# First mixer's input projection cut along K into 4, 5 and 7 tiles for every piece, with earlier parts written back into PSUM by ScalarE

## The chip, the core and the metric

One core of one Trainium2 chip runs the whole program. The metric is the device time of one execution in microseconds (us), lower is better. PE stands for TensorE, DVE for VectorE, ACT for ScalarE, POOL for GpSimd and SP for SyncE, whose queue issues nearly all loads.

## What is computed

Two decoder layers over 256 tokens of width 2048, batch 1, all in fp32. Each mixer and each feed-forward part starts from a normalised and modulated input, and the modulation is itself a matrix product with the conditioning vector `c`:

```python
cond = jax.nn.silu(c)
for i in range(DEPTH):                                   # 2 layers
    mod = (cond @ w_mod[i] + b_mod[i])[:, None, :]       # w_mod[i] is 2048 x 12288
    sh_m, sc_m, g_m, sh_f, sc_f, g_f = jnp.split(mod, 6, axis=-1)
    h = rmsnorm(x, norm_mix[i]) * (1.0 + sc_m) + sh_m
    y = gla_mixer(h, ...) if i % 2 == 0 else fox_mixer(h, ...)
    x = x + (1.0 + g_m) * y
    h = rmsnorm(x, norm_ffn[i]) * (1.0 + sc_f) + sh_f
    x = x + (1.0 + g_f) * conv_ffn(h, ...)
return rmsnorm(x, norm_final)

def gla_mixer(h, w_in, w_gate, b_gate, g_norm, w_out):   # the first mixer
    q, k, v, r, a = split(h @ w_in, widths 1024, 1024, 2048, 2048, 16)
    log_alpha = log_sigmoid(a @ w_gate + b_gate) / 16
    ...                                                  # chunked gated linear attention over q, k, v
    return (rmsnorm(o) * silu(r)) @ w_out
```

So the first mixer cannot multiply K rows 128k to 128k+127 of `w_in` before the same rows of `sc_m` and `sh_m` are known, and those need the matching columns of `w_mod`: 1 MB of `w_mod` for each of the two, for each of the 16 tiles of K.

## The kernel before

A weight tile is 128 rows of K by 1024 columns, 512 KB. Every tile goes the same way: SP loads it into the `ring` pool, ACT writes its rounded copy `wh` (L120), DVE writes the remainder `wl` (L124), and PE multiplies it in three products, `wh` by the high part of `h`, `wh` by its low part, `wl` by the high part: 24 matmuls of 256 columns (L602 to L604, the function `stream_a`), or 12 of 512 columns for the pieces `v0` and `v1` (L638 to L640, `stream_b`). `wh` and `wl` have AHEAD + 1 = 4 buffers each. So the cast of tile n waits until PE has finished tile n - 4, and at most three tiles wait converted.

`make_h` produces one K tile of `h`: DVE multiplies `x` by the token scale (L517), ACT writes the high part (L518), DVE computes the same affine in fp32 (L519) and subtracts (L520) for the low part. The modulation is summed on DVE, a multiply-add for each 128 rows of `w_mod` (L266, L268, `mod_tasks`, queued in `bg` and spread over the tiles by `set_pace`), then transposed, reduced and added up by a small matmul (L278, L279, L295, L311). For the first four K tiles of `h` it is summed on PE instead (`early_sum`, L1246, `early_finish`, L1252 and L1255), so that the first mixer can start; while PE waits for those loads it runs matmuls on the constant `fill` (L1283).

The first mixer's input projection (`gla`, `gla_rest`) has seven pieces: q, k, v0, v1, r0, r1 of 1024 columns and the narrow piece a of 16. Along K it runs in this order: q, k, v0 over K tiles 0 to 3; then `finish_late`, which sums `sh_m` for tiles 4 to 7 on PE; then q, k, v0 over tiles 4 to 7; then a, v1, r0, r1 over tiles 0 to 7; then all seven over tiles 8 to 15. PSUM has six banks in the pool `psA` for them, a piece takes four. When a piece has run a block, `fold` moves its four banks to SBUF: the first time ACT copies them, later DVE adds them to what is there.

Engines run their instructions in program order. The order on each engine is set by a scheduler from the order in the code and the dependences; `tc.issue_after` pins an instruction behind another. `psM` is a pool of two more PSUM banks for everything small.

Of the kernel before, what the change touches and what calls it, by code (L numbers as in the profile page):

```python
# [18 lines left out]
P = 128  # L19
# [16 lines left out]
SLOAD = 12  # L36
BACK = 1
STAGE = 3
FREE = 0
PEND = 3  # L40
BLOCKS = (8, 8)
HEAD = 4
HEADED = ('q', 'k', 'v0')
# [10 lines left out]
GP0 = 0.7  # L54
# [3 lines left out]
N0, N5 = 4, 5  # L58
BG0, BG1 = 0.95, 0.45
# [13 lines left out]
def kernel(  # L73
# [20 lines left out]
    order = {"v": None, "t": None}  # L94
# [20 lines left out]
    def split_w(src, moving, after=None):  # L115
# [4 lines left out]
        nc.scalar.copy(out=hi, in_=src)  # L120
# [71 lines left out]
    nc.vector.tensor_scalar_mul(vec[:, r0["qn"]:r0["qn"] + 1], vec[:, r0["qn"]:r0["qn"] + 1], float(P) ** -0.5)  # L192
# [40 lines left out]
    startup = {"loads": [], "left": SLOAD}  # L233

    def after_startup(on=True):
        es = ExitStack()
        if on and startup["left"] > 0 and len(startup["loads"]) >= BACK:
            startup["left"] -= 1
            es.enter_context(tc.issue_after(startup["loads"][-BACK]))
        return es  # L240

    def mod_tasks(l, key, f0=0, fn=D, wide=False, defer=False, turn=False):
# [8 lines left out]
        def chunk(c0, kt, st):  # L251
            def load():
                st[kt] = bigt([P, per, width], "wm") if wide else ringt([P, per, width], "wm")
                src = w_mod[l, kt * P:(kt + per) * P, s * D + c0:s * D + c0 + width]
                with after_startup():
                    nc.sync.dma_start(out=st[kt], in_=src.rearrange("(k p) m -> p k m", p=P))
# [241 lines left out]
    def make_h(l, kind):  # L498
# [12 lines left out]
        def make(m):  # L511
# [7 lines left out]
            nc.vector.tensor_scalar(out=t, in0=t, scalar1=sc, scalar2=sh, op0=ALU.mult, op1=ALU.add)  # L519
# [31 lines left out]
    def next_w(kt, cols, hold=None):  # L551
# [4 lines left out]
        if i < STAGE:  # L556
            run, look = min(run, STAGE - i), 1
        split_to(min(i + 1 + run, len(plan)), look)
        return splits.popleft()

    def split_to(end, look=LOOK):
        while fetched["split"] < end:
            while fetched["load"] < min(fetched["split"] + look, len(plan)):
# [4 lines left out]
                for c0, cn in cols_:  # L568
                    if nk_ == 1:
                        with after_startup():  # L570
                            nc.sync.dma_start(out=wt[:, o:o + cn], in_=w_[kt_ * P:(kt_ + 1) * P, c0:c0 + cn])
                        o += cn
                    else:
                        nc.sync.dma_start(out=wt[:, :nk_ * cn].rearrange("p (k r) -> p k r", r=cn),
                                          in_=w_[kt_ * P:(kt_ + nk_) * P, c0:c0 + cn]
                                          .rearrange("(k p) r -> p k r", p=P))
# [16 lines left out]
    def stream_a(kts, cols, rhs, done=None):  # L593

        ps = banks()
        held = []

        def mms(m, k, wh, wl, rh, rl):
            first, last = k == kts[0], k == kts[-1]
# [6 lines left out]
        for k in kts:  # L606
# [6 lines left out]
            for m in range(8):  # L613
                mms(m, k, wh, wl, rh, rl)
# [12 lines left out]
    def stream_b(kts, c0, lhs):  # L627
        ps = [b.rearrange("p j t -> p (j t)") for b in banks()]
        for k in kts:
            lh, ll = lhs(k)  # L630
            wh, wl = next_w(k, [(c0, 1024)])
            first, last = k == kts[0], k == kts[-1]
            for tt in range(TT):
                ts_ = slice(tt * P, (tt + 1) * P)
                for hf in range(2):
                    hs_ = slice(hf * 512, (hf + 1) * 512)
                    o = ps[tt * 2 + hf]
                    nc.tensor.matmul(o, lh[:, ts_], wh[:, hs_], start=first, stop=False)  # L638
                    nc.tensor.matmul(o, ll[:, ts_], wh[:, hs_], start=False, stop=False)  # L639
                    nc.tensor.matmul(o, lh[:, ts_], wl[:, hs_], start=False, stop=last)  # L640
# [45 lines left out]
    def gla(l, h, finish_late):  # L686
# [3 lines left out]
        def piece(key, kts, c0):  # L690
            if key == "a":
                return narrow(kts, c0, RANK, h)
            if key[0] == "v":
                return stream_b(kts, c0, h)
            return [p.rearrange("p j t -> p (j t)") for p in stream_a(kts, [(c0, 1024)], h)]

        def fold(key, ps):
# [9 lines left out]
            new = key not in parts  # L707
            if new:
                parts[key] = bigt([P, 4, 512], key)
            for b in range(4):  # L710
                dst = parts[key][:, b, :]
                if new:
                    nc.scalar.copy(out=dst, in_=ps[b])
                else:
                    nc.vector.tensor_tensor(out=dst, in0=dst, in1=ps[b], op=ALU.add)
# [6 lines left out]

        run(HEADED, ALL[:HEAD])
        drain_bg()
        finish_late()
        run(HEADED, ALL[HEAD:BLOCKS[0]])
        run([key for key, _ in pieces if key not in HEADED], ALL[:BLOCKS[0]])
        drain_bg()
        kts = ALL[BLOCKS[0]:]
        return kts, pieces, piece, fold, parts  # L730

    def gla_rest(l, kts, pieces, piece, fold, parts):
# [3 lines left out]
        nc.sync.dma_start(out=wg[RANK:RANK + 1, :], in_=gla_b_gate)  # L736
# [646 lines left out]
```

## Time and profile before

| | |
|---|---|
| time, median of 3 runs | 2430.47 us (2429.18 to 2430.49) |
| the profiled execution | 2429.0 us, of which the span of the trace 2427.0 us |
| first matmul of the first mixer | 43.66 us after the start of the span |
| PE busy, over the span | 98% |
| DVE, ACT busy | 79%, 52% |
| mean granted TensorE clock | 0.994 |

All times of the trace count from the start of the span. A PE that is shown as busy is not a PE at its peak, since matmuls are pipelined: at full clock the matmuls of 256 columns start every 0.113 us although each is shown with 0.28 us, so 24 of them, a tile, take 2.72 us. An idle time in brackets stands before the instruction, with what ended it.

### The profile page before, as it was taken

Reading aid. Unit: us, or ns where it says so; the run is one execution under the profiler, and the core shown is the slowest. Engines: PE = TensorE matmul, PEld = TensorE weight load, DVE = VectorE, ACT = ScalarE, POOL = GpSimd, SP = SyncE. Lnnn points to the kernel's source line nnn. Section 1 sums busy time; section 2 is a strip of 40 time slices with the busy share of each in tenths; the row PEclk is TensorE's granted clock in tenths of the full one; section 3 lists DMA queues with packets and bytes.
Section 4 is the critical chain, followed back from the end, with each engine's and each line's share of the span. In section 5 each row is a group of like instructions: output and inputs, shape, how many; then the busy total and the mean of one; then the engine's idle time right before and its main releaser. Section 6 shows DMA issues by size and latency. Waiting matters only on the chain.

```text
span 2427.0 us, 46850 instructions
## 1 busy us (share of the span) xinstructions
PE 2384.6 (98%) x19127; PEld 2285.0 (94%) x19131; DVE 1922.6 (79%) x2609; ACT 1252.4 (52%) x1671; POOL 16.2 (1%) x35
## 2 busy tenths in 40 slices
PE   6999999899999999999999999999999999999998
PEld 4898899899999999999988889999999999999998
DVE  4898989888789999986687998877776767777544
ACT  4447454445556665543454455545555555565433
POOL 0000000000000000000000000000000000000000
PEclk9999999999999999999999999999999999999999
DMA  9986968898668988998589887686777777756552
GB/s 376 374 303 222 328 223 312 297 343 293 195 200 297 318 305 311 326 315 314 164 298 314 299 272 251 215 296 228 235 235 228 240 227 236 232 195 217 191 191 104
DMA packets 188148, 638.31 MB, mean 263 GB/s; under 512 B 23705, under 2 KB 24715, under 8 KB 187548
## 3 DMA queue, kind: packets, MB, share of 16 engines
q1 hardware_dynamic: 186968, 634.12, 76.9%
q8 instruction: 149, 2.44, 0.4%
q10 hardware_dynamic: 964, 1.20, 0.1%
q14 instruction: 67, 0.55, 0.1%
HBM read 633.14 MB, written 2.10 MB: 262 GB/s over the span
## 4 chain that ended last, share of the span: by engine, by line
PE 95%; DVE 3%; DMA 1%; ACT 1%; issue 1%; DVEq 0%; SPq 0%
PE pa L604 25%; PE pa L603 25%; PE pa L602 25%; PE pa L640 5%; PE pa L639 5%; PE pa L638 5%; DMA wm<-in_w_mod_dram 1%; DVE wl L124 1%; PE pe L1246 0%; PE pm L473 0%; DVE acc L268 0%; PE pm L846 0%; PE pm L868 0%; PE pm L1057 0%; PE pt L288 0%
## 5 line engine op out<-in xcount | busy, mean ns | idle before, releaser
L120 ACT CAST wh<-w 128x1024 fp32r<-128x1024 f32 x819 | 856.4, 1049 | 1001.8 <-PE pa L603 707.9
L124 DVE TENSOR_TENSOR wl<-w,wh 128x1024 fp32r<-128x1024 f32 x819 | 995.8, 1218 | 408.8 <-ACT wh L120 403.6
L603 PE MATMUL pa<-h,wh 128*128 128x256 f32 x3584 | 990.8, 278 | 3.9 <-DVE h L520 3.9
L602 PE MATMUL pa<-h,wh 128*128 128x256 f32 x3584 | 987.7, 278 | 2.1 <-ACT h L518 2.1
L604 PE MATMUL pa<-h,wl 128*128 128x256 f32 x3584 | 987.3, 278 | 1.2 <-DVE wl L124 1.2
L603 PEld LDWEIGHTS pa<-h,wh 128*128 128x128 f32 x3584 | 675.3, 189 | 5.1 <-DVE h L520 4.9
L602 PEld LDWEIGHTS pa<-h,wh 128*128 128x128 f32 x3584 | 672.3, 188 | 4.9 <-ACT h L518 2.3
L604 PEld LDWEIGHTS pa<-h,wl 128*128 128x128 f32 x3584 | 672.8, 189 | 1.6 <-DVE wl L124 1.5
L603 PE MATMUL pa<-op,wh 128*128 128x256 f32 x1920 | 526.3, 276 | 0.0
L602 PE MATMUL pa<-op,wh 128*128 128x256 f32 x1920 | 526.3, 277 | 0.0
L604 PE MATMUL pa<-op,wl 128*128 128x256 f32 x1920 | 518.5, 276 | 0.3 <-DVE wl L124 0.3
L268 DVE SCALAR_TENSOR_TENSOR acc<-wm,cT,acc 128x1024 f32<-128x1024 f32 (+1 forms) x345 | 433.2, 1256 | 1.0 <-DMA wm<-in_w_mod_dram 0.3
L603 PEld LDWEIGHTS pa<-op,wh 128*128 128x128 f32 x1920 | 360.5, 188 | 0.0
L602 PEld LDWEIGHTS pa<-op,wh 128*128 128x128 f32 x1920 | 360.2, 188 | 0.0
L604 PEld LDWEIGHTS pa<-op,wl 128*128 128x128 f32 x1920 | 355.4, 188 | 0.5 <-DVE wl L124 0.5
L639 PE MATMUL pa<-wh,h 128*128 128x512 f32 x512 | 200.2, 392 | 0.0
L638 PE MATMUL pa<-wh,h 128*128 128x512 f32 x512 | 198.0, 391 | 0.0
L640 PE MATMUL pa<-wl,h 128*128 128x512 f32 x512 | 189.5, 393 | 0.0
L638 PEld LDWEIGHTS pa<-wh,h 128*128 128x128 f32 x512 | 96.1, 188 | 19.4 <-issue 0.2
L640 PEld LDWEIGHTS pa<-wl,h 128*128 128x128 f32 x512 | 95.9, 188 | 19.5
L639 PEld LDWEIGHTS pa<-wh,h 128*128 128x128 f32 x512 | 96.1, 188 | 19.0
L1109 ACT ACTIVATE y<-u,cw 128x256 f32<-128x256 f32 x176 | 101.6, 599 | 6.7 <-DVE act L1125 4.1
(263 smaller groups left out, 1315.0 us busy)
## 6 DMA issues: line engine op xcount, KB each, us to landing
wm<-in_w_mod_dram SPq DMA_DIRECT2D x320, 512.0 KB, 5.2
w<-in_ffn_w_up_dram SPq DMA_DIRECT2D x320, 512.0 KB, 4.5
w<-in_ffn_w_down_dram SPq DMA_DIRECT2D x176, 512.0 KB, 4.4
w<-in_fox_w_in_dram SPq DMA_DIRECT2D x128, 512.0 KB, 5.2
w<-in_gla_w_in_dram SPq DMA_DIRECT2D x96, 512.0 KB, 6.0
wm<-in_w_mod_dram SPq DMA_DIRECT2D x32, 1024.0 KB, 10.7
w<-in_gla_w_out_dram SPq DMA_DIRECT2D x32, 512.0 KB, 5.5
w<-in_ffn_w_up_dram SPq DMA_DIRECT2D x64, 256.0 KB, 4.5
```

Source lines behind the costliest of these rows:

```text
L120: nc.scalar.copy(out=hi, in_=src)
L124: order["v"] = nc.vector.tensor_tensor(out=lo, in0=src, in1=hi.bitcast(F32), op=ALU.subtract).ins
L268: nc.vector.scalar_tensor_tensor(out=st["a"], in0=wt[:, j, :], scalar=col, in1=st["a"], op0=ALU.mult, op1=ALU.add)
L602: nc.tensor.matmul(o, wh[:, ms], rh, start=(first and m % 2 == 0), stop=False, skip_group_check=True)
L603: nc.tensor.matmul(o, wh[:, ms], rl, start=False, stop=False, skip_group_check=True)
L604: nc.tensor.matmul(o, wl[:, ms], rh, start=False, stop=last, skip_group_check=True)
L638: nc.tensor.matmul(o, lh[:, ts_], wh[:, hs_], start=first, stop=False)
L639: nc.tensor.matmul(o, ll[:, ts_], wh[:, hs_], start=False, stop=False)
L640: nc.tensor.matmul(o, lh[:, ts_], wl[:, hs_], start=False, stop=last)
L1109: nc.scalar.activation(y, u, AF.Identity, scale=cw[:, l * 3 + 2, r:r + 1], bias=cw[:, 6 + l, r:r + 1])
```

## The change

Every piece now runs all three blocks of K, of 4, 5 and 7 tiles: q, k, v0, v1, r0, r1, a in the first two blocks, q, a, k, v0, v1, r0, r1 in the third. In the second and third block a piece starts by ACT copying its parts from SBUF into the four PSUM banks (`preload`); the matmuls accumulate on them, and `fold` is an ACT copy every time. The first two tiles of such a piece run over the first two banks, then over the other two. `sh_m` of tiles 4 to 7 is no longer summed on PE: the modulation of the next block is summed on DVE during the block before, must be drained one tile before its end, and the first `h` of the next block are requested behind its last wide tile (`hooks`). The two token loads go first, the loads of SP are chained in code order (`sync_load`), the transposes of the small vectors and of `b_mod` move behind the token sum. In `make_h` the fp32 affine of K tiles 3 and up is done by ACT (L532) instead of DVE, in all four places where `h` is made. Some numbers of pace change with it.

```diff
-SLOAD = 12
-BACK = 1
+SLOAD = 48
 STAGE = 3
+NEAR = 20
-BLOCKS = (8, 8)
+BLOCKS = (4, 5, 7)
 HEAD = 4
-HEADED = ('q', 'k', 'v0')
+STARTS = (0, 4, 9, 16)
+ORDERS = (("q", "k", "v0", "v1", "r0", "r1", "a"),) * 2 + (("q", "a", "k", "v0", "v1", "r0", "r1"),)
-GP0 = 0.7
+GP0 = 0.8
-N0, N5 = 4, 5
-BG0, BG1 = 0.95, 0.45
+EASE, N5 = 3, 5
+BG0, BG1 = 0.95, 0.75
...
+    def sync_load(out, in_):
+        with ExitStack() as es:
+            if startup["left"] > 0 and startup["last"] is not None:
+                startup["left"] -= 1
+                es.enter_context(tc.issue_after(startup["last"]))
+            startup["last"] = nc.sync.dma_start(out=out, in_=in_).ins
...
             hot = nc.scalar.activation(hi, t, AF.Identity, scale=sc, bias=sh).ins
-            nc.vector.tensor_scalar(out=t, in0=t, scalar1=sc, scalar2=sh, op0=ALU.mult, op1=ALU.add)
+            if m < 3:
+                nc.vector.tensor_scalar(out=t, in0=t, scalar1=sc, scalar2=sh, op0=ALU.mult, op1=ALU.add)
+            else:
+                nc.scalar.activation(t, t, AF.Identity, scale=sc, bias=sh)
             ins = nc.vector.tensor_tensor(out=lo, in0=t, in1=hi.bitcast(F32), op=ALU.subtract).ins
...
+    def preload(ps, base):
+        if base is not None:
+            for b in range(4):
+                nc.scalar.copy(out=ps[b], in_=base[:, b, :])
...
-            first, last = k == kts[0], k == kts[-1]
+            first, last = base is None and k == kts[0], k == kts[-1]
...
+            if base is not None and k in kts[:2]:
+                held.append((k, wh, wl, rh, rl))
+                for args in held if k == kts[1] else ():
+                    for m in range(4):
+                        mms(m, *args)
+                while k == kts[1] and held:
+                    args = held.pop(0)
+                    for m in range(4, 8):
+                        mms(m, *args)
+            else:
+                for m in range(8):
+                    mms(m, k, wh, wl, rh, rl)
...
             for b in range(4):
-                dst = parts[key][:, b, :]
-                if new:
-                    nc.scalar.copy(out=dst, in_=ps[b])
-                else:
-                    nc.vector.tensor_tensor(out=dst, in0=dst, in1=ps[b], op=ALU.add)
+                nc.scalar.copy(out=parts[key][:, b, :], in_=ps[b])
...
-        run(HEADED, ALL[:HEAD])
-        drain_bg()
-        finish_late()
-        run(HEADED, ALL[HEAD:BLOCKS[0]])
-        run([key for key, _ in pieces if key not in HEADED], ALL[:BLOCKS[0]])
-        drain_bg()
-        kts = ALL[BLOCKS[0]:]
+        for n_ in range(len(BLOCKS) - 1):
+            run(ORDERS[n_], ALL[STARTS[n_]:STARTS[n_ + 1]])
+        kts = ALL[STARTS[-2]:]
...
-        pace["side"], pace["sacc"] = 1.0, 0.0
-        fold("q", piece("q", kts, off["q"]))
+        pace["side"], pace["sacc"] = 1.4, 0.0
+        fold("k", piece("k", kts, off["k"]))
         drain_side()
...
-    for args in todo[:2]:
-        startup["loads"].append(early_load(*args))
     xs = fetch_x()
-    for args in todo[2:WIDE]:
-        startup["loads"].append(early_load(*args))
+    for args in todo[:WIDE]:
+        early_load(*args)
     load_x(xs)
+    with tc.issue_after(order["s"]):
+        turn_rows()
...
+        if m in STARTS[:-2]:
+            n_ = STARTS.index(m) + 1
             for key in ("sc_m", "sh_m"):
-                queue(mod_tasks(0, key, BLOCKS[0] * P, BLOCKS[1] * P, wide=True))
-            set_pace(6 * BLOCKS[0] - HEAD * len(HEADED) - N0)
+                queue(mod_tasks(0, key, STARTS[n_] * P, BLOCKS[n_] * P, wide=True))
+            n_use = 6 * BLOCKS[n_ - 1]
+            set_pace(n_use - EASE)
+            end = fetched["use"] + n_use + (m > 0)
+            hooks[end - 1] = drain_bg
+            hooks[end] = lambda: h(STARTS[n_])
```

What this does to the order of instructions is shown at three places.

The first is SP's queue at the start of the program. `xtok` are the tokens, `wm` the tiles of `w_mod` (the eight of 128x4x512 are those that PE sums for the first four K tiles), `w` the tiles of `w_in`. Before:

```order
L159 DMA crow_104<-in_c_dram 16x128
L1239 DMA wm_145<-in_w_mod_dram 128x4x512
L1239 DMA wm_147<-in_w_mod_dram 128x4x512
L423 DMA xtok_149<-in_x_dram 128x2048
L423 DMA xtok_150<-in_x_dram 128x2048
L1239 DMA wm_153<-in_w_mod_dram 128x4x512
```

And now:

```order
L164 DMA crow_104<-in_c_dram 16x128
L433 DMA xtok_135<-in_x_dram 128x2048
L433 DMA xtok_136<-in_x_dram 128x2048
L248 DMA wm_139<-in_w_mod_dram 128x4x512
L248 DMA wm_141<-in_w_mod_dram 128x4x512
L248 DMA wm_143<-in_w_mod_dram 128x4x512
```

The tokens stand ahead of all `w_mod` loads; in both programs the eighth of those is followed by the first `w` tiles.

The second place is the end of a block of K, where `h` of the next block is made. Before, at the only such end that is followed by all seven pieces (K tile 7 to 8), ACT has the cast of the tile that waits for the block's last wide tile (`wh_1930`), the last copy of r1's parts (`r_302_1903`) and then `h`; DVE has the sums of the modulation (`mod`), one `wl`, the affine and the low part:

```order
L713 COPY r_302_1903<-pa_1643 128x512
L120 CAST wh_1930<-w_1738 128x1024
L713 COPY r_302_1903<-pa_1644 128x512
L518 ACTIVATE h_1912<-hn_1913,mod 128x256
L518 ACTIVATE h_1912<-hn_1918,mod 128x256
L518 ACTIVATE h_1912<-hn_1923,mod 128x256
```

```order
L311 TENSOR_TENSOR mod<-pm_1837,bm 32x8 x4
L124 TENSOR_TENSOR wl_1931<-w_1738,wh_1930 128x1024
L519 TENSOR_SCALAR hn_1913<-hn_1913,mod 128x256
L519 TENSOR_SCALAR hn_1918<-hn_1918,mod 128x256
L520 TENSOR_TENSOR h_1912<-hn_1913,h_1912 128x256
```

Now, at the end of the first block (K tile 3 to 4), ACT has, from the cast that waits for r1's last tile (`wh_1152`) on, three `h`, the four copies of r1, a fourth `h`, a second cast (`wh_1181`), and only then the affine that the low part of `h` needs:

```order
L125 CAST wh_1152<-w_991 128x1024
L528 ACTIVATE h_1128<-hn_1129,mod 128x256
L528 ACTIVATE h_1128<-hn_1134,mod 128x256
L528 ACTIVATE h_1128<-hn_1139,mod 128x256
L750 COPY r_197_1144<-pa_980 128x512
L750 COPY r_197_1144<-pa_981 128x512
L750 COPY r_197_1144<-pa_982 128x512
L750 COPY r_197_1144<-pa_983 128x512
L528 ACTIVATE h_1128<-hn_1191,mod 128x256
L125 CAST wh_1181<-w_993 128x1024
L532 ACTIVATE hn_1129<-hn_1129,mod 128x256
```

DVE at the same place has both `wl` ahead of the first low part (`h_1128<-hn_1129`):

```order
L318 TENSOR_TENSOR mod<-pm_1092,bm 32x5 x4
L129 TENSOR_TENSOR wl_1153<-w_991,wh_1152 128x1024
L742 COPY aT<-pm_1149 16x256
L129 TENSOR_TENSOR wl_1182<-w_993,wh_1181 128x1024
L533 TENSOR_TENSOR h_1128<-hn_1129,h_1128 128x256
```

On PE the narrow piece a (12 matmuls, L691 to L693) stands behind r1, then two matmuls of q that need the high part of `h` alone (L621), then one that needs the low part (L622).

A second `wl`, with its cast, has come ahead of the first low part of `h` on DVE, and the affine has moved from DVE to ACT, behind that cast. The end of the second block (K tile 8 to 9) has the same shape, with four `h` ahead of the second cast on ACT and four matmuls of q ahead of the low part on PE.

The third place is ACT in the middle of the first feed-forward part, where the second half of its K starts (K tile 7 to 8); `u` takes the copies of the four banks. Before, DVE has there:

```order
L311 TENSOR_TENSOR mod<-pm_6597,bm 32x8 x4
L124 TENSOR_TENSOR wl_6636<-w_6469,wh_6635 128x1024
L519 TENSOR_SCALAR hn_6673<-hn_6673,mod 128x256
L519 TENSOR_SCALAR hn_6678<-hn_6678,mod 128x256
L520 TENSOR_TENSOR h_6672<-hn_6673,h_6672 128x256
```

Now the affines stand on ACT:

```order
L528 ACTIVATE h_6775<-hn_6776,mod 128x256
L528 ACTIVATE h_6775<-hn_6781,mod 128x256
L528 ACTIVATE h_6775<-hn_6786,mod 128x256
L528 ACTIVATE h_6775<-hn_6827,mod 128x256
L1162 COPY u_6766<-pa_6507 128x512
L1162 COPY u_6766<-pa_6508 128x512
L532 ACTIVATE hn_6776<-hn_6776,mod 128x256
L532 ACTIVATE hn_6781<-hn_6781,mod 128x256
```

The two affines stood on DVE (L519) behind one `wl`; now they stand on ACT (L532) behind four `h` and two copies, and DVE's low part waits for them.

More of the change, by code (lines that the diff above doesn't have):

```diff
@@ L93 @@
     cnt = [0]
-    order = {"v": None, "t": None}
+    order = {"v": None, "f": None}
     def nm(s):
@@ L119, in split_w @@
         lo = split.tile([P, WCOLS], F32R, tag="wl", name=nm("wl"))[:, o2:o2 + n_]
-        nc.scalar.copy(out=hi, in_=src)
+        with ExitStack() as es:
+            if order["f"] is not None:
+                es.enter_context(tc.issue_after(order["f"]))
+                order["f"] = None
+            nc.scalar.copy(out=hi, in_=src)
         with ExitStack() as es:
@@ L232 @@
     fin = {}
[L233 to L240, printed above, removed]
+    startup = {"last": None, "left": SLOAD}
+    def sync_load(out, in_):
+        with ExitStack() as es:
+            if startup["left"] > 0 and startup["last"] is not None:
+                startup["left"] -= 1
+                es.enter_context(tc.issue_after(startup["last"]))
+            startup["last"] = nc.sync.dma_start(out=out, in_=in_).ins
     def mod_tasks(l, key, f0=0, fn=D, wide=False, defer=False, turn=False):
@@ L254, in load @@
                 src = w_mod[l, kt * P:(kt + per) * P, s * D + c0:s * D + c0 + width]
-                with after_startup():
-                    nc.sync.dma_start(out=st[kt], in_=src.rearrange("(k p) m -> p k m", p=P))
+                sync_load(st[kt], src.rearrange("(k p) m -> p k m", p=P))
             def f():
@@ L625, in stream_a, with stream_b, mms @@
         return ps
-    def stream_b(kts, c0, lhs):
+    def stream_b(kts, c0, lhs, base=None):
         ps = [b.rearrange("p j t -> p (j t)") for b in banks()]
+        preload(ps, base)
+        held = []
+        def mms(tt, k, wh, wl, lh, ll):
+            first, last = base is None and k == kts[0], k == kts[-1]
+            ts_ = slice(tt * P, (tt + 1) * P)
+            for hf in range(2):
+                hs_ = slice(hf * 512, (hf + 1) * 512)
+                o = ps[tt * 2 + hf]
+                nc.tensor.matmul(o, lh[:, ts_], wh[:, hs_], start=first, stop=False, skip_group_check=True)
+                nc.tensor.matmul(o, ll[:, ts_], wh[:, hs_], start=False, stop=False, skip_group_check=True)
+                nc.tensor.matmul(o, lh[:, ts_], wl[:, hs_], start=False, stop=last, skip_group_check=True)
         for k in kts:
@@ L631, in stream_b @@
             wh, wl = next_w(k, [(c0, 1024)])
[L632 to L640, printed above, removed]
+            held.append((k, wh, wl, lh, ll))
+            if base is None or k != kts[0]:
+                for tt in range(TT):
+                    for args in held:
+                        mms(tt, *args)
+                held.clear()
             tick()
@@ L1230 @@
     plan_ffn(1)
-    load_bmod()
     early = {}
@@ L1251, in early_finish @@
         rows_ = t2("er")
-        nc.scalar.copy(out=rows_, in_=early.pop((key, f0)))
+        order["f"] = nc.scalar.copy(out=rows_, in_=early.pop((key, f0))).ins
         pt = misc()
@@ L1274 @@
         if i + WIDE < len(todo):
-            startup["loads"].append(early_load(*todo[i + WIDE]))
-        summed = early_sum(*args)
+            early_load(*todo[i + WIDE])
+        with tc.issue_after(order["s"]):
+            summed = early_sum(*args)
         if args[2] == 3:
```

81 lines of the change are left out of this document (34 added, 47 removed).

## The prediction

> **What bounds the kernel now.** I read the page's busy times and chain first, then the stages up to the end of the first mixer, then PE's rows at each stop. The page:
>
> ```profile
> PE 2384.6 (98%) x19127; PEld 2285.0 (94%) x19131; DVE 1922.6 (79%) x2609; ACT 1252.4 (52%) x1671; POOL 16.2 (1%) x35
> PE 95%; DVE 3%; DMA 1%; ACT 1%; issue 1%; DVEq 0%; SPq 0%
> ```
>
> PE holds 95% of the chain that ends last, and the change leaves its matmuls as they are. So only stops of PE can be won or lost, and each other engine counts only where PE waits for it. The stages (columns: stretch, length, busy time and count of PE, PEld, DVE, ACT, POOL, then PE's granted clock, DMA share, GB/s):
>
> ```profile
> 0.00:43.66 43.66, 24.67 (x133) 10.54 (x134) 12.10 (x40) 15.33 (x26) 0.96 (x7) 0.96 0.98 369
> 43.66:80.66 37.00, 35.77 (x244) 33.31 (x248) 32.69 (x44) 19.96 (x27) 0.00 (x0) 0.91 1.03 389
> 80.66:91.35 10.69, 9.25 (x63) 6.23 (x64) 7.72 (x21) 4.59 (x9) 0.00 (x0) 0.84 0.81 271
> 91.35:190.30 98.95, 98.95 (x729) 93.25 (x728) 90.45 (x96) 41.15 (x47) 0.23 (x2) 1.00 0.89 325
> 190.30:197.20 6.90, 4.59 (x24) 4.27 (x24) 6.80 (x20) 5.26 (x10) 0.00 (x0) 0.75 0.50 154
> 197.20:445.00 247.80, 247.46 (x2010) 234.68 (x2010) 222.07 (x284) 134.19 (x207) 3.38 (x10) 1.00 0.83 288
> ```
>
> Three places lose time ahead of 445 us: the start, the stop at 80.66 where `sh_m` of tiles 4 to 7 is summed on PE, and the stop at 190.30 where `h` of tiles 8 to 15 begins. Between them PE never idles. A stop costs clock too: 0.84 of 10.69 us is 1.7 us lost, 0.75 of 6.90 us is 1.7.
>
> **What is removed: the start.** PE's rows and what DMA had moved by 17.73 and by 30.0 us:
>
> ```profile
> 17.73 1.91 PE L1246 MATMUL pe<-wm,cz 128*32 128x512 f32 x2 [6.18 <-DMA wm<-in_w_mod_dram]
> DMA packets 2520, 5.87 MB, mean 331 GB/s; under 512 B 194, under 2 KB 500, under 8 KB 2264
> DMA packets 4902, 10.62 MB, mean 354 GB/s; under 512 B 265, under 2 KB 571, under 8 KB 4646
> 38.64 0.67 PE L473 MATMUL pm<-ss,onesD 128*128 128x256 f32 x2 [3.29 <-DVE ss L466]
> 43.66 1.22 PE L602 MATMUL pa<-h,wh 128*128 128x256 f32 x4 [1.22 <-ACT h L518]
> 47.02 0.58 PE L604 MATMUL pa<-h,wl 128*128 128x256 f32 x1 [1.23 <-DVE wl L124]
> ```
>
> The loads are at their rate all the time; what is late is the token sum at 38.64, behind the tokens. With the tokens first it is done early, and the last of the eight `w_mod` loads decides. The tokens, the eight loads and the small ones are 10.6 MB, moved by 30.0 us in either order. The third `w_mod` load is complete after 5.4 MB; it released PE when 5.87 MB had moved, so a load counts about 1.1 us after its bytes: 31.1. Then four matmuls of the sum (1.1), ACT's copy of it (0.6), two casts of 1.0 that stand ahead of `h` on ACT (33.8, then 34.8; the second tile lands just before), and the first `h` (0.6): 35.4 instead of 43.66, **8.3 us won** (7 to 10). From first matmul to first `wl` product I keep the 3.4 us of the last two rows, and the half clock after it.
>
> **Removed: the stop at 80.66.**
>
> ```profile
> 80.58 3.64 PE L1246 MATMUL pe<-wm,cz 128*32 128x512 f32 x32
> 84.16 0.40 PE L295 MATMUL pm<-red,quad 128*128 128x16 f32 x2
> 84.93 1.05 PE L1255 MATMUL pm<-ones,er 128*128 128x1 f32 x8 [0.38 <-ACT er L1252]
> 86.87 0.74 PE L602 MATMUL pa<-h,wh 128*128 128x256 f32 x4 [0.89 <-ACT h L518]
> ```
>
> From 80.58 to 86.87 are 6.3 us, and 1.7 of clock: **8.0 won**. DVE takes the sums over. Its 32 multiply-adds of 640 columns in the first block are 0.8 each by the 1.28 for 1024 (last DVE row below): 26 us, with 24 `wl` of 1.2 and 8 for `h` and ends 63 us, beside PE's 24 tiles of 2.72 us, 65 us. In the second block 32 of 1.1 and 30 `wl` and 8: 80 beside 83. So DVE just keeps up; nothing is taken for it, up to 8 us in the range. Loads: 23 MB in the first block's 70 us are 330 GB/s against 389 in the second row of the stages, so hidden; w_mod comes in 8 more DMAs, a comes in one more, on an SP queue with room.
>
> **The old end of a block, and the two new ones.** PE, ACT and DVE at 190:
>
> ```profile
> 190.25 0.30 PE L295 MATMUL pm<-red,quad 128*128 128x32 f32 x2
> 192.41 0.38 PE L652 MATMUL pm<-h,wh 128*128 128x256 f32 x1 [1.86 <-ACT h L518]
> 193.72 0.58 PE L653 MATMUL pm<-h,wh 128*128 128x256 f32 x1 [0.45 <-DVE h L520]
> 190.33 1.04 ACT L120 CAST wh<-w 128x1024 fp32r<-128x1024 f32 x1
> 191.28 0.58 ACT L713 COPY r<-pa 128x512 f32<-128x512 f32 x1
> 191.76 2.08 ACT L518 ACTIVATE h<-hn,mod 128x256 fp32r<-128x256 f32 x4
> 184.06 1.28 DVE L268 SCALAR_TENSOR_TENSOR acc<-wm,cT,acc 128x1024 f32<-128x1024 f32 x1
> 190.74 0.69 DVE L311 TENSOR_TENSOR mod<-pm,bm 32x8 f32<-32x8 f32 x4
> 191.46 1.23 DVE L124 TENSOR_TENSOR wl<-w,wh 128x1024 fp32r<-128x1024 f32 x1
> 192.60 0.73 DVE L519 TENSOR_SCALAR hn<-hn,mod 128x256 f32<-128x256 f32 x2
> 193.25 0.75 DVE L520 TENSOR_TENSOR h<-hn,h 128x256 fp32r<-128x256 f32 x2
> ```
>
> Everything hangs on T, the end of r1's last matmul: the cast needs its buffer, the small matmul (L295) stands behind it on PE. The old end: idle 1.9 and 0.45 and clock 1.7, **4.1 won**.
>
> The new ones are counted with the same prices (starts on ACT and DVE are closer than durations: cast 1.0, h 0.5, copy 0.5, `wl` 1.15, low part 0.4) along the order shown ahead. End of block one: cast to T+1.05, three `h` to 2.7, r1's four copies to 4.7, a fourth `h` to 5.2, second cast to 6.2, affine to 6.75; DVE's second `wl` to 7.4, then the first low part, 7.8. PE has the small matmul, the 12 of piece a and two of q until T+1.85: 5.9 idle, and 1.6 for clock (half a window less or more): **7.5 lost**. End of block two: cast 1.05, `wl` 2.3, the sums behind it 3.0, four `h` 5.1, second cast 6.1, `wl` 7.3, low part 7.7; PE has 2.35 of work: 5.35 and 1.6, **7.0 lost**. Both together 14.5, between 8.2 (each like the old end) and 19 (half clock for two windows, a copy that waits).
>
> The Trainium skill (TensorE: Matmul & The Clock Gate, What's actually happening) lets the clock fall to half after an idle window of about 3.4 us; here pauses of 1.86 and 0.45 us were enough for 0.75, so the measurement decides. By the page the pause of 2.5 us below would keep its clock, and the sum be 0.8 us less.
>
> **ACT's added work.** A preload (SBUF to PSUM) is not in the trace; the nearest row is the copy out of PSUM, 0.58. 48 preloads and 48 more copies out are some 50 us over 230, and DVE loses 36 adds. A piece starts on two banks filled ahead, which last two tiles' half, 2.7 us; ACT needs two copies and two preloads, 2.0 us, for the others, begun 2 us before the end. So 0 (between -1, less work in DVE's queue, and 12, 1 us at each of 12 starts); I take 0, as four copies fit with the spacing of 0.5.
>
> The gate's stage (log-sigmoid) is fuller: 14 casts, 12 copies and preloads and the same six table loads and functions now fall on one piece of 7 tiles, 40 us of ACT in 42:
>
> ```profile
> 220.33 1.28 ACT L682 ACT_TABLE_LOAD   x1
> 222.72 1.23 DVE L683 SCALAR_TENSOR_TENSOR la<-la,le 128x1024 f32<-128x1024 f32 x1
> 224.00 0.82 PE L764 MATMUL pm<-mgla,la 128*128 128x128 f32 x5 [0.34 <-DVE la L683]
> ```
>
> PE waited 0.34 for the second half of `la`; ACT has in that piece four copies and three preloads more ahead of it, 3.5 us, less the room it had: **1.6 lost** (0 to 5).
>
> The middle of the first feed-forward part:
>
> ```profile
> 595.81 2.08 ACT L518 ACTIVATE h<-hn,mod 128x256 fp32r<-128x256 f32 x4
> 597.79 1.05 ACT L1131 COPY u<-pa 128x512 f32<-128x512 f32 x2
> 597.01 0.50 PE L602 MATMUL pa<-h,wh 128*128 128x256 f32 x3
> 597.74 0.38 PE L603 MATMUL pa<-h,wh 128*128 128x256 f32 x1 [0.22 <-DVE h L520]
> ```
>
> The affine now starts behind those copies, at 598.8, ends at 599.4, the low part at 599.8: 2.1 us after 597.74, a pause of 2.5, and a half chance of half clock, 0.8: **2.9 lost** (0 to 4). At other places with more on ACT (the last scores, the start of the second mixer) I take **1.4** (0 to 4). The Trainium skill (ScalarE: Activation LUTs, Rules for kernel authors) gives adds and multiplies to VectorE; the rows agree, 0.37 a piece on DVE against 0.5 on ACT. By it the 2.1 us here would stay unpaid, while at the two ends the low part waits for `wl` longer than for the affine.
>
> **The sum:** won 8.3 + 8.0 + 4.1 = 20.4; lost 7.5 + 7.0 + 1.6 + 2.9 + 1.4 = 20.4. Nothing is left: the profiled execution's 2429.0 stays, and it stood 1.5 under the median, so 2430 for the median.
>
> **Rivals.** Short ends: the order hides no second cast in time, each new end costs the old one's 4.1. For it: the old end kept its second cast out of the chain. Against it: the order. 6.3 less, 2424. Hidden ACT work: PE lives on its three converted tiles, 8.2 us, in the gate's stage and the feed-forward part; 5.9 less, 2424.5. Both: 2418. DVE as the bound: with PE never idle it was busy 90.45 of 98.95, 91%; if it cannot go beyond that, 63 and 80 us need 69 and 88, 8 us more, 2438; it decides once its share must pass 95%. Late preloads: each of 12 piece starts waits 1 us, 2442; against it the 2.7 us of cover.
>
> **Numbers.** Within 0.2% (4.9 us, about what a measurement of this kernel can tell from no change): 0.42, own range 2426 to 2435. Short ends 0.19, hidden ACT work 0.15: faster 0.34. DVE 0.16, preloads 0.08: slower 0.24. The range 2418 to 2438 takes in all but late preloads and tails.
>
> **What the next profile would show.** The first L621 near 35.4, the token sum before 25. No L1270 behind the first tile. Near 105 and 196 two stops of PE, released by DVE's low part (L533), of 6 and of 1.7 and 3.6 us, each followed by half clock. One stop of 2 to 3 us at the feed-forward middle. Wrong if PE passes those ends with stops under 3 us, if L621 waits for `wl` (L129) inside the blocks, or for preloads (L609).

## The result and the profile after

| | time, median (range) | ratio to before, 95% interval |
|---|---|---|
| before | 2430.48 us (2429.18 to 2430.52) | |
| changed | 2444.10 us (2442.14 to 2447.30) | 1.0059 (1.0041 to 1.0076) |

The change makes the kernel 0.6% slower, 13.6 us. The profiled execution took 2444.97 us, with a span of 2443.3, 16.3 more than before. The page, first PE's busy time and the chain by engine:

```profile
PE 2388.1 (98%) x19089; PEld 2292.1 (94%) x19093; DVE 1901.7 (78%) x2548; ACT 1326.6 (54%) x1819; POOL 16.1 (1%) x35
PE 95%; DVE 2%; ACT 2%; DMA 1%; issue 1%; SPq 0%; DVEq 0%; ACTq 0%
```

They say hardly more than before: a loss of 0.6% is not seen in shares. What finds it is progress: the time at which PE has done n weight tiles (24 matmuls of 256 columns, or 12 of 512), counted in the two traces.

| tiles done | place | before | changed | changed less before |
|---|---|---|---|---|
| 0 | first matmul of the first mixer | 43.66 | 38.72 | -4.9 |
| 24 | the removed stop lies behind | 121.51 | 109.22 | -12.3 |
| 96 | end of the input projection | 361.39 | 359.65 | -1.7 |
| 104 | half of the output projection's first piece | 383.68 | 383.81 | +0.1 |
| 108 | four tiles on | 394.56 | 412.86 | +18.3 |
| 132 | first feed-forward part has begun | 476.71 | 489.60 | +12.9 |
| 180 | its middle is past | 608.27 | 624.77 | +16.5 |
| end | span | 2427.0 | 2443.3 | +16.3 |

The stages of the changed kernel in which PE stood (stretch, length, busy time and count of PE, PEld, DVE, ACT, POOL, then PE's granted clock, DMA share, GB/s), and the one ahead of the longest stop:

```profile
0.00:38.72 38.72, 23.48 (x132) 10.97 (x133) 12.19 (x39) 15.12 (x26) 0.96 (x7) 0.96 0.98 363
108.10:124.00 15.90, 10.48 (x68) 10.16 (x67) 8.12 (x18) 11.51 (x21) 0.00 (x0) 0.79 0.96 358
201.20:215.00 13.80, 9.34 (x54) 8.85 (x53) 9.04 (x21) 12.50 (x23) 0.23 (x2) 0.75 0.40 116
359.60:383.80 24.20, 22.65 (x194) 22.06 (x194) 23.58 (x30) 13.53 (x19) 0.00 (x0) 1.00 0.88 307
383.80:406.00 22.20, 12.02 (x54) 10.95 (x53) 16.22 (x27) 7.11 (x22) 0.00 (x0) 0.62 0.54 211
```

The start and the two block ends were forecast as the places where PE stands. The last row was not: between 383.8 and 406 PE is busy 12 of 22 us, at a clock of 0.62. Below, "lost" in a stretch is the sum of PE's start-to-start times beyond the usual one of the same matmul (0.113 us for 256 columns). Its rows on PE, and on DVE the second token scale of the mixer, from the copy of its variance (`pvar`) through two of its 13 small steps to the diagonal (`dg`) that PE waits for:

```profile
392.34 0.80 PE L424 MATMUL pm<-dg,ones 128*128 128x128 f32 x2 [8.26 <-DVE dg L422]
395.65 1.12 PE L306 MATMUL pm<-ident,acc 128*128 128x128 f32 x4 [1.23 <-ACT pm L310]
```

```profile
351.81 0.15 DVE L916 COPY pvar<-pm 128x2 f32<-128x2 f32 x1
354.53 0.16 DVE L403 TENSOR_SCALAR rv<-pvar 128x4 f32<-128x4 f32 x1
382.44 0.15 DVE L411 TENSOR_TENSOR rt<-rt,grs 128x4 f32<-128x4 f32 x1
391.81 0.15 DVE L416 SCALAR_TENSOR_TENSOR grs<-rt,grs 128x4 f32<-128x4 f32 x1
392.00 0.48 DVE L422 TENSOR_SCALAR dg<-ident,grs 128x128 f32<-128x128 f32 x2
```

This is `rsqrt` for heads 2 and 3 (`scale_of(2)`, L403 to L416): 13 steps of 0.16 us, each needing the one before, 2 us of work that took from 354.5 to 392.0. What DVE did from the variance to that diagonal, by groups (busy time, mean ns), first changed, then before, where the same stretch is 334.4 to 358.6:

```profile
L275 DVE SCALAR_TENSOR_TENSOR acc<-wm,cT,acc 128x1024 f32<-128x1024 f32 x13 | 16.6, 1278 | 2.0 <-DMA wm<-in_w_mod_dram 1.8
L129 DVE TENSOR_TENSOR wl<-w,wh 128x1024 fp32r<-128x1024 f32 x13 | 15.7, 1213 | 0.0
L410 DVE TENSOR_TENSOR rt<-rv,grs 128x4 f32<-128x4 f32 x3 | 0.5, 152 | 0.0
```

```profile
L124 DVE TENSOR_TENSOR wl<-w,wh 128x1024 fp32r<-128x1024 f32 x7 | 8.5, 1217 | 1.1 <-ACT wh L120 1.1
L268 DVE SCALAR_TENSOR_TENSOR acc<-wm,cT,acc 128x1024 f32<-128x1024 f32 x3 | 3.8, 1277 | 0.0
```

In the changed kernel 13 sums of the modulation and 13 `wl` stand in DVE's queue between the variance and that diagonal, before it was 3 and 7. The queue was full: DVE was busy 23.58 of the 24.20 us ahead of the stop (fourth row of the stages). PE's broadcast of the scale stands behind tile 104, and the second half of the output projection's first operand behind it.

The Trainium skill (TensorE: Matmul & The Clock Gate, Step-by-step: what each phase is for) says that PE alone of the engines reorders, and that only in its weight loads. The trace agrees: a step of 0.15 us starts only when what stands ahead of it has run, though PE waited 8.26 us for the end of the chain.

The block ends, forecast at 6 us and at 1.7 and 3.6 (PE's stops, and for the first ACT and DVE):

```profile
116.97 0.58 PE L622 MATMUL pa<-h,wh 128*128 128x256 f32 x1 [5.42 <-DVE h L533]
203.16 0.41 PE L302 MATMUL pm<-red,quad 128*128 128x28 f32 x2 [1.68 <-DVE red L286]
209.88 0.39 PE L622 MATMUL pa<-h,wh 128*128 128x256 f32 x1 [2.78 <-DVE h L533]
114.28 1.04 ACT L125 CAST wh<-w 128x1024 fp32r<-128x1024 f32 x1
115.22 1.59 ACT L532 ACTIVATE hn<-hn,mod 128x256 f32<-128x256 f32 x3
115.36 1.23 DVE L129 TENSOR_TENSOR wl<-w,wh 128x1024 fp32r<-128x1024 f32 x1 [3.19 <-ACT wh L125]
116.50 1.09 DVE L533 TENSOR_TENSOR h<-hn,h 128x256 fp32r<-128x256 f32 x3
```

The low part (L533) comes behind the second cast, the affine (L532) and the second `wl`, as the order had it; 8.4 us are lost from 105 to 125 and 7.9 from 198 to 216, stops and lower clock together.

### The profile page after: what moved, and what is told of

It reads as the page before. It is cut to its first block, busy times and chain, and to the rows that moved or that the text cites. A ratio compares the mean times of both kernels' runs of the same rounds, so it can differ in the third digit from the quotient of the medians.

```text
span 2443.3 us, 46907 instructions
## 1 busy us (share of the span) xinstructions
PE 2388.1 (98%) x19089; PEld 2292.1 (94%) x19093; DVE 1901.7 (78%) x2548; ACT 1326.6 (54%) x1819; POOL 16.1 (1%) x35
## 4 chain that ended last, share of the span: by engine, by line
PE 95%; DVE 2%; ACT 2%; DMA 1%; issue 1%; SPq 0%; DVEq 0%; ACTq 0%
PE pa L622 25%; PE pa L623 25%; PE pa L621 25%; PE pa L668 5%; PE pa L669 5%; PE pa L667 5%; DVE wl L129 1%; DMA wm<-in_w_mod_dram 1%; PE pe L1270 0%; DVE acc L275 0%; ACT wh L125 0%; PE pm L483 0%; PE pm L877 0%; DMA xtok<-in_x_dram 0%; PE pm L1088 0%
## 5 line engine op out<-in xcount | busy, mean ns | idle before, releaser
L622 PE MATMUL pa<-h,wh 128*128 128x256 f32 x3584 | 993.7, 278 | 13.3 <-DVE h L533 13.3
L621 PE MATMUL pa<-h,wh 128*128 128x256 f32 x3584 | 991.6, 278 | 2.2 <-ACT h L528 1.3
L622 PEld LDWEIGHTS pa<-h,wh 128*128 128x128 f32 x3584 | 677.4, 189 | 15.1 <-DVE h L533 14.8
L621 PEld LDWEIGHTS pa<-h,wh 128*128 128x128 f32 x3584 | 675.3, 189 | 5.4 <-issue 1.5
L622 PE MATMUL pa<-op,wh 128*128 128x256 f32 x1920 | 529.4, 277 | 1.8 <-DVE op L549 1.8
L621 PE MATMUL pa<-op,wh 128*128 128x256 f32 x1920 | 528.9, 278 | 0.4 <-ACT op L548 0.2
L623 PE MATMUL pa<-op,wl 128*128 128x256 f32 x1920 | 524.8, 277 | 0.0
L275 DVE SCALAR_TENSOR_TENSOR acc<-wm,cT,acc 128x1024 f32<-128x1024 f32 (+2 forms) x360 | 444.3, 1235 | 10.7 <-DMA wm<-in_w_mod_dram 9.4
L622 PEld LDWEIGHTS pa<-op,wh 128*128 128x128 f32 x1920 | 362.0, 189 | 2.3 <-DVE op L549 2.3
L621 PEld LDWEIGHTS pa<-op,wh 128*128 128x128 f32 x1920 | 361.2, 189 | 1.1 <-ACT r L750 0.6
L669 PE MATMUL pa<-wl,h 128*128 128x512 f32 x512 | 194.4, 392 | 0.0
```

The lines of the kernel that those rows point to most:

```text
L275: nc.vector.scalar_tensor_tensor(out=st["a"], in0=wt[:, j, :], scalar=col, in1=st["a"], op0=ALU.mult, op1=ALU.add)
L621: nc.tensor.matmul(o, wh[:, ms], rh, start=(first and m % 2 == 0), stop=False, skip_group_check=True)
L622: nc.tensor.matmul(o, wh[:, ms], rl, start=False, stop=False, skip_group_check=True)
L623: nc.tensor.matmul(o, wl[:, ms], rh, start=False, stop=last, skip_group_check=True)
```

## The experiments

All are compared with the kernel before, run beside them. Theory Q: the new stop is the chain of small steps in DVE's queue. Rivals: DVE is the bound there (B), or the pieces ahead are late (P).

**The second scale by ScalarE.** In the changed kernel:

```diff
-            return lambda: rsqrt(grs[:, 2 * hd:2 * hd + 4], pvar[:, 2 * hd:2 * hd + 4], 1.0 / 512.0, 4)
+            if hd == 0:
+                return lambda: rsqrt(grs[:, 0:4], pvar[:, 0:4], 1.0 / 512.0, 4)
+            return lambda: nc.scalar.activation(grs[:, 4:8], pvar[:, 4:8], AF.Abs_reciprocal_sqrt, scale=1.0 / 512.0,
+                                                bias=epsc)
```

> Edit to the changed kernel: the token scale of heads 2 and 3 of the first mixer comes from one ScalarE activation (Abs_reciprocal_sqrt of the variance) in place of the 13 small DVE steps of rsqrt (L403 to L416); nothing of the later arithmetic is changed, the scale itself is a little less exact. Theory Q (queue): the stop of PE at 383.81 us, 15.7 us lost with its clock and 2.5 more just before, exists because each of those 13 steps, 0.16 us long, stands behind a wl of 1.22 and a sum of 1.28 on DVE, so that the chain takes 40 us. Then the stop is gone, what is lost between 356 and 408 falls from 18.2 to under 2, and the time is 2428 (2425 to 2432), the lower end if the start of the first feed-forward part keeps its gain. Rival B (DVE is the bound there, 23.6 busy of 24.2 us): the 13 steps are only 2 us of DVE, so 2441 to 2443 and a stop of some 14 us elsewhere. Rival P (the pieces before it, the variance 17 us later than before): the scale is still late by part, a stop of 5 us or more stays, 2433 to 2438.

2436.94 us, 1.0028 (1.0017 to 1.0039), 7.2 under the changed kernel. All that PE still waits for between 356 and 410 us, in the view of waits (us in total, times, longest):

```profile
PE pm L306 <- DVE oT L930: 0.8, 1, 0.8
```

Lost there: 1.8 us instead of 18.2. That is Q, and against P: with the variance as late as in the changed kernel (353.79, there 351.81), nothing is left of the stop. It is against B too: the rest of DVE's work is the same, and no stop of some 14 us comes elsewhere. The time missed my range by 5 us. One reason is the start of the first feed-forward part, which loses 10.2 us (453 to 483), about as in the kernel before (9.3), where the changed kernel lost only 4.5: PE waits 3.9 us there for DVE's token sum `ss`, a wait that the changed kernel does not have:

```profile
457.29 0.70 PE L483 MATMUL pm<-ss,onesD 128*128 128x256 f32 x2 [3.91 <-DVE ss L476]
```

While PE stands for 16 us, DVE works on, and is ahead of its sums when the feed-forward part needs it. About a third of the stop is paid back there. The other reason is spread: the profiled execution took 2434.05 us, the fastest of seven that reach up to 2440.26.

**Old numbers of pace.** In the changed kernel. GP0 sets how many small tasks of the mixer go behind a tile of r0, BG1 how many sums of the modulation go behind a tile of r0 and r1:

```diff
-GP0 = 0.8
+GP0 = 0.7
-BG0, BG1 = 0.95, 0.75
+BG0, BG1 = 0.95, 0.45
```

> Edit to the changed kernel: two numbers of pace back to their old values, GP0 0.8 to 0.7 and BG1 0.75 to 0.45 (sums of the modulation per tile while r0 and r1 run). In the order on DVE the 13 steps then end behind the wl of tile 103 instead of 111. Theory Q: the stop near 384 is gone or under 3 us, 2427 to 2432, with all the rest of the change in place. Rival B (DVE as the bound): the sums that are held back come later, the stop only moves, 2440 to 2444. Rival P (late variance because of seven-tile pieces and preloads): half of the stop stays, 2435 to 2438.

2436.52 us, 1.0027 (1.0017 to 1.0037). Lost between 356 and 410: 5.1, but only 0.2 of them behind 376: the stop at 384 is gone. The rest is another wait, 2.5 us at 362 for the first operand of the output projection (`op`), which the changed kernel has as well, with 1.3 us. It is slower than I said because this wait is longer and because, as in the run before, the start of the feed-forward part takes some of the stop back.

**The numbers of pace alone, in the kernel before.** The same lines the other way:

```diff
-GP0 = 0.7
+GP0 = 0.8
-BG0, BG1 = 0.95, 0.45
+BG0, BG1 = 0.95, 0.75
```

> The kernel before with only two numbers of pace as in the change: GP0 0.7 to 0.8 and BG1 0.45 to 0.75. In the order on DVE the 13 small steps of the second scale then end behind the wl of tile 107 instead of 98, and PE's broadcast of that scale stands behind tile 104 of the output projection, as in the changed kernel. Theory Q (the queue): PE stops there, near 384 us, for 3 to 10 us and loses clock: 2436 to 2444, with blocks, preloads and start as before. Rival P (the stop needs seven-tile pieces, preloads or the later variance): under 2 us, 2429 to 2432.

2432.63 us, 1.0010 (1.0001 to 1.0019). PE, at the same place of the output projection, with the old blocks and no preload:

```profile
385.13 0.49 PE L414 MATMUL pm<-dg,ones 128*128 128x128 f32 x2 [1.21 <-DVE dg L412]
386.46 0.80 PE L414 MATMUL pm<-dg,ones 128*128 128x128 f32 x2 [0.84 <-DVE dg L412]
388.88 1.09 PE L299 MATMUL pm<-ident,acc 128*128 128x128 f32 x4 [1.63 <-DVE acc L268]
```

9.1 us are lost there, and the feed-forward part again starts with 4.5 instead of 9.3, so the time is under my range. Of the 18.2 us of the changed kernel 15.7 are lost behind 376, at this stop. The two numbers make 9.1 there by themselves, and without them 0.2 are left, with the variance late all the same (350.68). So the stop needs the fuller queue. That the later variance makes the other 6.6 is the likely reading, and no run shows it alone; which of the two numbers does more was not tried either.

**Blocks of 4, 4 and 8 tiles.**

```diff
-BLOCKS = (4, 5, 7)
+BLOCKS = (4, 4, 8)
-STARTS = (0, 4, 9, 16)
+STARTS = (0, 4, 8, 16)
```

> Edit to the changed kernel: blocks of K of 4, 4 and 8 tiles instead of 4, 5 and 7. In the order on DVE the 13 steps of the second scale then stand together, behind the wl of tiles 94 and 95. Theory Q: no stop near 384, lost between 356 and 408 under 2 us; the two block ends still cost 7 to 8.5 us each: 2427 (2424 to 2432). Rival B: DVE has the same sums to do, 2438 or more. A rival to my reading of the block ends: the second end is shorter with a block of four tiles ahead of it, or longer because DVE has 24 tiles instead of 30 for sums of 1024 columns (32 of 1.28 and 24 wl of 1.22 are 70 us beside 65 of PE), then PE stops for the sums near 170 to 180 us for 5 us or more and the time is 2432 to 2436.

2433.93 us, 1.0016 (1.0008 to 1.0025). Lost between 360 and 412: 0.4, so here too the chain in one place takes the stop away. A new one comes at the end of the second block:

```profile
198.88 0.64 PE L302 MATMUL pm<-red,quad 128*128 128x32 f32 x2 [12.20 <-DVE red L286]
```

```profile
111.00:186.40 75.40, 69.97 (x493) 65.91 (x493) 64.44 (x74) 54.20 (x85) 0.00 (x0) 0.95 1.00 385
186.40:199.00 12.60, 0.40 (x4) 0.20 (x2) 12.24 (x13) 3.51 (x7) 0.03 (x1) 0.60 0.20 49
```

Of the stages, the first row is the block, the second the stop. In four tiles of K the sums of 1024 columns do not fit, as the last rival said, with 12 us where it had 5 or more. DVE was busy 64 of 75 us and DMA all of it at 385 GB/s. From 111 to 199 us DVE never waits for a load of `w_mod`; what it waits for is ACT's casts, with its sums in the queue behind the `wl` (view of waits), so the loads did not hold it up:

```profile
DVE wl L129 <- ACT wh L125: 9.8, 6, 4.5
```

**The first affines on DVE.** In the changed kernel:

```diff
-            if m < 3:
+            if m < 3 or m in (4, 8, 9):
```

> Edit to the changed kernel: the fp32 affine of K tiles 4, 8 and 9 is done by DVE again, all others from 3 up stay on ACT. In the order on DVE the first low part of h then stands ahead of the second wl at both block ends. My theory of the ends: the low part waits for the affine behind the second cast on ACT and for the second wl on DVE; then the stop at 111.27 falls from 5.6 to about 1.5 us and the one at 206.69 from 3.1 to about 0.5, with half a clock window less each, and the middle of the first feed-forward part loses 0.5 instead of 4.1: 10 us less, 2434 (2431 to 2438), the stop near 384 unchanged. Rival: the ends wait for h's high part and the copies, not for the affine: under 3 us less, 2441 to 2444.

2434.25 us, 1.0015 (1.0006 to 1.0024), 9.9 under the changed kernel, as forecast. Lost at the ends: 4.4 (105 to 125) and 3.5 (196 to 214) for 8.4 and 7.9, at the feed-forward middle 0.6 for 4.1. The stop near 384 stays, with 14.0 lost from 376 to 412 for 15.7. PE at the first end:

```profile
115.02 0.39 PE L622 MATMUL pa<-h,wh 128*128 128x256 f32 x1 [1.34 <-DVE h L533]
118.99 0.39 PE L621 MATMUL pa<-h,wh 128*128 128x256 f32 x1 [2.28 <-ACT pa L609]
```

The low part is early, and the next in ACT's queue is late: q's preload (L609) behind the second cast and two affines.

**Both edits.** The second scale by ScalarE and the first affines on DVE together.

> The changed kernel with both edits at once: the second token scale from one ScalarE activation, and the affine of K tiles 4, 8 and 9 on DVE. Each alone brought 7.2 and 9.9 us (2436.9 and 2434.3). If they are two stops with nothing in common, 2427 (2425 to 2430), under the kernel before; lost between 105 and 125 us some 4.5, between 356 and 408 some 3.5, at the start of the first feed-forward part 9 again. Rival: a DVE with too little room takes part of it back elsewhere: 2430 to 2434.

2421.50 us, 0.9965 (0.9952 to 0.9977): 22.6 under the changed kernel, and faster than before. The two edits alone brought 7.2 and 9.9, so the two causes at least add up. The profiled executions (2434.05, 2434.93 and 2424.15 against 2444.97) gave 10.9, 10.0 and 20.8; that the medians give more than the sum lies within their spread. PE passes tile 96 at 352.87 and tile 108 at 388.93, 36.1 us for 53.2 in the changed kernel.

**Both edits, no preload.** As the last, with `base = None` in `piece`, so that the first two tiles of a piece no longer run over two banks at a time, and in `fold`:

```diff
+            new = key not in parts
...
-            for b in range(4):
-                nc.scalar.copy(out=parts[key][:, b, :], in_=ps[b])
+            for b in range(4):
+                dst = parts[key][:, b, :]
+                if new:
+                    nc.scalar.copy(out=dst, in_=ps[b])
+                else:
+                    nc.vector.tensor_tensor(out=dst, in0=dst, in1=ps[b], op=ALU.add)
```

> As the run with both edits, but no piece starts on its earlier parts: PSUM starts empty, the parts are added by DVE at the end of a piece (one add of 0.64 us for each bank, 24 in the second block, 28 in the third, less ScalarE's 48 copies in and 48 out). My term for the preloads was 0. If they cost nothing, DVE's adds make it slower: in the second block 70 us of DVE and 15 of adds stand against 82 of PE, so the sums end late and PE stops there for 4 to 8 us: 3 to 9 us over the run with both edits. Rival: the preloads cost PE 2 us at the first block end (2.3 waited for one in the run with the affines) and more at others: 2 us or more under the run with both edits.

2436.93 us, 1.0028 (1.0017 to 1.0038), 15.4 over the run with both edits, where I had 3 to 9. The second block, and PE's wait at its end (us in total, times, longest):

```profile
118.00:197.10 79.10, 78.89 (x573) 74.17 (x574) 77.47 (x96) 29.23 (x31) 0.00 (x0) 1.00 0.96 343
```

```profile
PE pm L302 <- DVE red L286: 11.8, 1, 11.8
```

DVE is busy 77.5 of 79.1 us and still late: this is what DVE as the bound looks like, and what keeps the changed kernel from it is that the parts are added up in PSUM and not by DVE. At the first block end the rival is right: 3.1 us are lost there for the 4.5 with preloads.

**The start alone.** In the kernel before:

```diff
-    for args in todo[:2]:
-        startup["loads"].append(early_load(*args))
     xs = fetch_x()
-    for args in todo[2:WIDE]:
+    for args in todo[:WIDE]:
...
-        summed = early_sum(*args)
+        with tc.issue_after(order["s"]):
+            summed = early_sum(*args)
```

> The kernel before with the start alone: both token loads ahead of all loads of w_mod, and the sums of w_mod on PE behind the token sum; all else as before. What the changed kernel gains at its start is 3.3 to 4.9 us (first matmul at 38.72 to 40.39 in five profiles against 43.66), not my 8.3. Theory: the eighth load of w_mod decides (counted at 34.6 in the changed kernel), and ScalarE's two casts stand ahead of the copy of its sum: first matmul at 37 to 39.5, 2425 (2423.5 to 2427). Rival: the later blocks lose it again, since q, k and v0 reach the stop at 80 us earlier than the sums there are loaded: 2429 to 2431.

2427.84 us, 0.9988 (0.9979 to 0.9997), 2.3 us under the kernel before. The first matmul comes at 42.99, only 0.7 us earlier than before:

```profile
14.41 0.39 PE L203 MATMUL pm<-ident,brow 96*128 96x96 f32 x1 [0.84 <-DMA brow<-in_b_mod_dram]
25.61 1.19 PE L473 MATMUL pm<-ss,onesD 128*128 128x256 f32 x2 [3.29 <-DVE ss L466]
39.28 1.06 PE L1246 MATMUL pe<-wm,cz 128*32 128x512 f32 x8
```

The tokens lie in SBUF, but their transposes stand behind those of `b_mod`, whose load comes at 14.4, the token sum at 25.6, and all eight sums of `w_mod` and the fill matmuls behind that. PE is never idle for long from there, and reaches the eighth sum at 39.28, where the kernel before, whose sums do not stand behind the token sum, reaches it at 32.37. So the tokens first and the sums behind them win almost nothing at the first matmul; where the other 1.6 us of the time come from, this run does not show. The change also moves the transposes of `b_mod`. The order of the loads alone, without the sums pinned behind the token sum, was not run.

**Fewer fill matmuls.** The run with both edits, and `KEEP` 5 to 1.

> The run with both edits (2421.5), and one fill matmul on PE behind each of the first three sums of the last four w_mod loads instead of five. In the changed kernel the eighth load has landed at 31.05 us, by the DMA events, as forecast, but PE comes to its sum at 34.56, because the eight sums stand behind the token sum of 19.89 and 15 fill matmuls of 0.25 stand between them. Theory (PE's own queue decides the start): 12 matmuls or 2.6 to 3.2 us less in that queue, first matmul of the first mixer 2.5 to 3.5 us earlier, at 36 to 37.5, and 2418.5 (2417 to 2420.5). Rival (the clock): with PE idle while it waits for the last two loads, the clock goes to half for more of the time from 36 to 55 us, and 2421 to 2424. Rival (the loads after all): the first matmul stays at 39 to 40, 2421.5.

2422.56 us, 0.9969 (0.9957 to 0.9980). The eighth sum and the first matmul, in the changed kernel, then here:

```profile
33.38 1.25 PE L1308 MATMUL pw<-fill 128*128 128x512 bf16 x5
34.56 1.06 PE L1270 MATMUL pe<-wm,cz 128*32 128x512 f32 x8
38.72 0.74 PE L621 MATMUL pa<-h,wh 128*128 128x256 f32 x4 [1.34 <-ACT h L528]
```

```profile
33.25 1.06 PE L1273 MATMUL pe<-wm,cz 128*32 128x512 f32 x8
37.41 0.74 PE L621 MATMUL pa<-h,wh 128*128 128x256 f32 x4 [1.33 <-ACT h L528]
```

The run to compare with is the one with both edits, whose clock over the first 30 us is 0.89 as here, and 0.94 in the changed kernel. The first matmul comes 2.45 us earlier than there (39.86), so PE's queue sets it. The clock is not what takes this back, since tile 24 is still passed 2.8 us earlier (107.76 for 110.57). At tile 28, behind the first block end, 1.4 us of it are left (126.12 for 127.51); at that end PE now waits 0.5 us for `red` and 1.5 for `h`. The spans of the two profiles are 2421.2 and 2422.4, the medians stand 1.1 us the other way, and no gain of the whole is shown.

**And two more numbers of pace.** As the last, with `EASE` 3 to 5 and `BG1` 0.75 to 0.6.

> As the last, and two numbers of pace more: EASE 3 to 5 (the sums for the next block spread over two tiles less) and BG1 0.75 to 0.6 (fewer sums beside r0 and r1). In the run with both edits PE waits 1.7 us at 200 us for the reduction of the sums, and loses 3 near 354 where the first operand of the output projection waits on DVE. If DVE has the room: these two go, 3 us less than the last run. Rival (DVE is full there, 88% busy in the second block): the sums push wl back and PE waits for wl instead, or the sums held back at 350 come at 440: no difference, or 1 to 3 us more.

2419.36 us, 0.9958 (0.9944 to 0.9971), the lowest median of all; its interval overlaps those of the last run and of the run with both edits, so a gain over them is not shown. Lost from 192 to 212: 2.5 for 3.6; PE no longer waits for `red`. Near 354 nothing changed: 1.7 us are lost from 345 to 400, against 1.8 in the run with both edits.

## Why the prediction was wrong, by its steps

- **The start, 8.3 won:** 4.9 in this profile, 3.3 to 4.9 in seven. The step that failed is "the last of the eight `w_mod` loads decides". By the DMA events of the trace the eighth load was complete at 31.05 us; I had 31.1. But PE came to its sum only at 34.56, behind seven other sums and 15 fill matmuls, all of which now stand behind the token sum of 19.89; the kernel before came to it at 32.37. From there to the first matmul it took 4.2 us, I had 4.3. I counted a queue as empty that the change itself had filled.
- **The stop at 80, 8.0 won:** right, 7.4 between the first matmul and tile 24. The sums on DVE and the loads were hidden in the first two blocks, but for the 1.68 us that PE waits for `red` at 203.
- **The old end, 4.1 won, and the new ones, 7.5 and 7.0 lost:** right in mechanism, which the run with the first affines on DVE shows, and near in size: 8.4 and 7.9. The stops themselves, by start-to-start times, were 5.6 and 1.8 and 3.1; the rest is clock, 2.8 and 3.0 for my 1.6.
- **Preloads at nothing:** right. No piece start waits for them in the changed kernel; the 2.3 us of the run with the first affines on DVE appear when the affine no longer hides them. Taking them away cost 15.4.
- **The feed-forward middle, 2.9 lost:** near, 3.6. PE waits there 0.89 us for a copy (L1162) and 1.06 for the low part, and the rest is clock. **The gate's stage, 1.6:** too much; PE waits 0.6 us there, and from 215 to 300 us the changed kernel loses 1.4 in all, 0.7 more than the old one.
- **"At other places with more on ACT I take 1.4":** this is the step that failed and decides the outcome. Behind "the last scores" lay the second token scale; the stop took 18.2 us between tiles 104 and 108, and 5.4 came back at the start of the feed-forward part. The term was put on the wrong engine, too: it is DVE's queue that makes PE wait, through two numbers of pace of the diff for which the prediction had no term, and probably through a variance that is ready 17 us later. The signs of being wrong that it named lay at the block ends, inside the blocks and at the preloads, and did not cover this place.

With the measured 4.9 for 8.3 the sum comes to 2432, and with the stop for the 1.4, less what it gave back, to 2444. Of the rivals, short ends did not occur; hidden ACT work about held in the gate's stage and not in the feed-forward part; late preloads gave 2442, close to the time by luck, for a reason that did not occur. DVE as the bound (2438) is a limit that the run without preloads reaches and the changed kernel does not in the first two blocks (72.06 of 83.20 us busy in the second). Ahead of the stop it was busy 97% of the time; what made PE wait there was still the place of the chain, since one activation in place of 2 us of DVE took the stop away.

## What to carry to other kernels

A chain of small dependent steps costs its place in the queue, not its 2 us: when the engine that runs it has a backlog, nearly every step waits for one or two long instructions (here 13 steps took 37.5 us), so follow each such chain to its consumer in the order of the changed kernel and count what stands between its steps. An edit that loads an engine more, or a number that sets a pace, is a term of its own, at every place that the engine feeds. And progress at fixed points of the work, side by side, finds a stop that shares of busy time do not show, and what is paid back later.

## What the runs showed of the hardware

Seven profiles with the same start have their first matmul between 38.72 and 40.39 us. The first 30 us of the changed kernel and of the run with both edits:

```profile
0.00:30.00 30.00, 16.80 (x90) 7.90 (x91) 11.69 (x35) 12.10 (x21) 0.96 (x7) 0.94 0.96 351
0.00:30.00 30.00, 16.53 (x80) 8.21 (x82) 11.70 (x35) 12.10 (x21) 0.96 (x7) 0.89 0.95 348
```

The granted clock is 0.94 in the one and 0.89 in the other, and the first matmul comes 1.1 us later in the second. Of this, 0.7 us stand already at the token sum (19.89 and 20.57), since the second half of the tokens landed at 8.98 and 9.67 us by the DMA events. From the token sum to the eighth sum of `w_mod` PE takes 14.67 and 15.13 us, 0.5 more at the lower clock. In the seven profiles this stretch is shortest where the clock from 20 to 34 us is highest (14.67 us at 0.88) and longest where it is lowest (15.70 us at 0.79, the run with the first affines on DVE): how fast PE's queue drains there depends on when the clock rises. The Trainium skill (TensorE: Matmul & The Clock Gate, What's actually happening) has the gate's window of 3.4 us run freely, so that the moment differs from run to run; these rows fit that.
